# Order of 512- and 256-column products inside a weight unit of a feed-forward layer (two-layer streaming-encoder trunk, Trainium2)

## The chip, the cores and the metric

One core of one Trainium2 chip runs the whole program. The time is the device time of one execution in microseconds; smaller is better. It is the median of several executions. Engines are called as in the profile: PE (TensorE products), PEld (TensorE weight loads), DVE (VectorE), ACT (ScalarE), POOL (GpSimd), SP (the engine that issues most DMAs).

## The reference

A trunk of two layers over 256 positions of width 1024. Each layer has two feed-forward blocks, a token mixer between them and a gated embedding at the end; all matrices are float32.

```
def swiglu(x, w13, w2):
    gate, up = jnp.split(x @ w13, 2, axis=-1)
    return (jax.nn.silu(gate) * up) @ w2
...
    for i in range(DEPTH):
        h = h + 0.5 * rms_norm(swiglu(rms_norm(h, g[0]), ffn_w13[i, 0], ffn_w2[i, 0]), g[1])
        ...
        h = h + 0.5 * rms_norm(swiglu(rms_norm(h, g[4]), ffn_w13[i, 1], ffn_w2[i, 1]), g[5])
        ...
```

Between the two feed-forward blocks of a layer stands its token mixer, a gMLP in layer 0 and an RWKV-7 in layer 1. So there are four feed-forward blocks, each with a 1024 x 5632 matrix `w13` (gate and up halves) and a 2816 x 1024 matrix `w2`.

## The kernel before

**Precision by two parts.** A float32 operand is kept as a high part, rounded to the type fp32r, and a low part, the rest. A product of two such operands is made of three: high by high, low by high, high by low. Weights arrive from memory in units of 128 x 1024 (512 KB); ACT casts a unit to its high part (line 154), DVE subtracts that from the raw unit to get the low part (line 156). Both parts stand in one slot of 2048 columns: `need(i)` hands out `wh` and `wl`, `release(i)` gives the slot back. `pump` runs this splitting ahead of the products, up to 12 units.

**A feed-forward block** is the function `ffn`. The 2816 inner columns are cut into `FC` = 11 chunks `c` of 256. For the chunks 0 and 1 the products are made by `A` with the activations as stationary operand. For the chunks 2 to 10 the function `AT` makes them transposed, with the weights as stationary operand and the activations moving. `Dn(c, b)` then multiplies a chunk's result with `w2` for one half `b` of the positions: 12 products of 512 columns through `mm3` (lines 178, 179 and 180: high by high, low by high, high by low), three at a time into one of two PSUM banks called `acc`. The loop over `c` calls `AT(c)` and then, from the chunk two before, `Dn(c - 2, 0)` and `Dn(c - 2, 1)`.

**Inside `AT`** a chunk has two halves `j`, each with two PSUM banks `ps[0]` (gate) and `ps[1]` (up) and two weight units `u`. A unit holds four blocks `q` of 128 rows of the sum. The activations stand in `xs[u]` so that for each block the 256 columns of the high part (one for each position) are followed by the 256 of the low part. One product of the high weights with all 512 columns therefore gives high by high in `ps[i][:, :T]` and high by low in `ps[i][:, T:]`, and one of the low weights with the first 256 columns adds low by high to `ps[i][:, :T]` (`T` = 256). That is 16 products to a unit, eight of 512 columns (line 400) and eight of 256 (line 401), each with its own load of 128 stationary columns. After both units ACT copies the second halves of the banks out (line 408) and DVE adds the first halves (line 409); a scaling, the SiLU and the split of the result follow (lines 412 to 417).

The program has 4 blocks x 9 chunks = 36 calls of `AT`, 144 weight units in them, and 1152 pairs of a 512- and a 256-column product. The order of the products on PE is the order in which the code is written. Other places of the program show chains of products of one size: the gate product of the embedding and the `z` and `acc` products (512 columns), and the spatial product `s` of the gMLP (256 columns, 12 products in a row), all through `mm3`.

Of the kernel before, what the change touches and what calls it, by code (L numbers as in the profile page):

```python
# [16 lines left out]
T = 256  # L17
NB = 2
KT = 8
# [41 lines left out]
class Trunk:  # L61
# [264 lines left out]
    def ffn(self, l, j, at, filler=None):  # L326
        nc = self.nc
        at13, at2 = at
        gcol = l * 8 + 4 * j
        xs, xT, rstd = [], [], [None, None]  # L330
# [57 lines left out]
        def AT(c):  # L388


            for j in range(2):
                ps = [self.bank("mm") for _ in range(2)]
                for u in range(2):
                    wh, wl = self.need(at13[c] + 2 * j + u)
                    for q in range(4):
                        k = 4 * u + q
                        x = xs[u][:, q * 512:(q + 1) * 512]
                        for i in range(2):
                            sl = slice(q * 256 + i * 128, q * 256 + i * 128 + 128)
                            nc.tensor.matmul(ps[i], lhsT=wh[:, sl], rhs=x, start=k == 0, stop=False)  # L400
                            nc.tensor.matmul(ps[i][:, :T], lhsT=wl[:, sl], rhs=x[:, :T], start=False, stop=k == KT - 1)  # L401
                    self.release(at13[c] + 2 * j + u)
                self.pump(1, self.room)
                z = self.small(512, "pn", 3)
                sg = self.small(256, "k1", 6)
                for i in range(2):
                    zi = z[:, i * T:(i + 1) * T]
                    nc.scalar.copy(zi, ps[i][:, T:])  # L408
                    nc.vector.tensor_tensor(zi, ps[i][:, :T], zi, op=ALU.add)  # L409
                self.unbank(*ps)  # L410
                z2 = z.rearrange("p (i t) -> p i t", i=2)
                nc.vector.tensor_tensor(z2, z2, rbc.unsqueeze(1).to_broadcast([128, 2, T]), op=ALU.mult)  # L412
                nc.scalar.activation(sg, z[:, :T], AF.Silu)
                nc.vector.tensor_tensor(sg, sg, z[:, T:], op=ALU.mult)
                hi, lo = hv(c)[:, 0, j, :], hv(c)[:, 1, j, :]
                nc.scalar.copy(hi, sg)
                nc.vector.tensor_tensor(lo, sg, hi.bitcast(F32), op=ALU.subtract)
# [24 lines left out]
        for c in range(2, FC):  # L442
            AT(c); P(1)
            if c == 2:
                TR(1, 1)
            if c < FC - 1:
                Dn(c - 2, 0); P(2)
                if c < FC - 2:
                    Dn(c - 2, 1); P(1)
# [1151 lines left out]
```

## Time and profile before

| | us |
|---|---|
| runs | 1216.73, 1217.44, 1223.06 (median 1217.44) |
| the profiled execution, its own time | 1223.09 |
| its span, first to last instruction | 1221.2 |
| PE busy | 1188.6 (97% of the span) |
| DVE busy | 839.2 (69%) |
| ACT busy | 652.3 (53%) |
| mean granted TensorE clock | 0.981 of full speed |

The profiled execution has 1.9 us outside its span. A busy figure is the union of the records of an engine; since products are pipelined, their records overlap, and the time that one product adds to a chain is read from the start of one record to the start of the next, not from a record's length.

### The profile page before, as it was taken

What the parts mean: (1) busy time and instruction counts of PE and PEld (TensorE: products, weight loads), DVE (VectorE), ACT (ScalarE), POOL (GpSimd) and SP (SyncE); (2) the same over time, 40 slices, a digit from 0 to 9 for tenths busy, and PEclk for the clock granted to TensorE, in tenths of its full rate; (3) what the DMA queues carried; (4) which work ended last, traced back from release to release, by engine and by line L of the source; (5) the groups of instructions that cost most, each with busy time, mean ns of one, the idle gap of its engine ahead of it and who ended that gap; (6) DMA issues with size and microseconds to landing.
All of it is one profiled execution on the core that took longest, in us unless ns stands there. A gap on an engine that the chain in (4) does not pass through costs nothing. (4 is left out here: it accounts for less than half of the span.)

```text
span 1221.2 us, 18852 instructions
## 1 busy us (share of the span) xinstructions
PE 1188.6 (97%) x7374; PEld 966.8 (79%) x7374; DVE 839.2 (69%) x1273; ACT 652.3 (53%) x1122; POOL 97.7 (8%) x109
## 2 busy tenths in 40 slices
PE   8999999999999999999999999989899899999997
PEld 6888888888888888887888886576575778888886
DVE  5886666686787667668766744699253988666663
ACT  6665556454575555468655522472161377555553
POOL 0000001000010000012000001300025420000011
PEclk8999999999999999999999999999789899999999
DMA  7886655655767666555766672103020358656510
GB/s 245 293 282 190 191 171 163 234 173 189 220 209 231 191 186 187 188 171 167 242 183 196 189 281 98 50 4 138 3 93 19 121 194 273 198 183 192 171 58 35
DMA packets 58778, 207.73 MB, mean 170 GB/s; under 512 B 6720, under 2 KB 7232, under 8 KB 58432
## 3 DMA queue, kind: packets, MB, share of 16 engines
q1 hardware_dynamic: 58688, 206.51, 52.4%
q8 instruction: 58, 0.95, 0.3%
q14 instruction: 32, 0.26, 0.1%
HBM read 205.44 MB, written 1.05 MB: 169 GB/s over the span
## 5 line engine op out<-in xcount | busy, mean ns | idle before, releaser
L156 DVE TENSOR_TENSOR w<-raw,w 128x1024 fp32r<-128x1024 f32 x335 | 407.9, 1223 | 160.3 <-ACT w L154 154.8
L154 ACT CAST w<-raw 128x1024 fp32r<-128x1024 f32 x340 | 357.4, 1055 | 185.2 <-PE mm L401 76.2
L400 PE MATMUL mm<-xT,w 128*128 128x512 f32 x1152 | 408.5, 399 | 0.0
L401 PE MATMUL mm<-xT,w 128*128 128x256 f32 x1152 | 323.4, 281 | 0.0
L400 PEld LDWEIGHTS mm<-xT,w 128*128 128x128 f32 x1152 | 216.4, 188 | 53.4
L401 PEld LDWEIGHTS mm<-xT,w 128*128 128x128 f32 x1152 | 217.6, 189 | 1.3
L178 PE MATMUL acc<-w,hT 128*128 128x512 f32 x352 | 138.7, 394 | 0.0
L180 PE MATMUL acc<-w,hT 128*128 128x512 f32 x352 | 137.6, 391 | 0.0
L179 PE MATMUL acc<-w,hT 128*128 128x512 f32 x352 | 137.2, 390 | 0.0
L408 ACT COPY pn<-mm 128x256 f32<-128x256 f32 x144 | 48.6, 373 | 87.9 <-PE mm L401 87.9
L409 DVE TENSOR_TENSOR pn<-mm,pn 128x256 f32<-128x256 f32 x144 | 54.7, 420 | 36.1 <-ACT pn L408 36.1
L180 PEld LDWEIGHTS acc<-w,hT 128*128 128x128 f32 x352 | 66.1, 188 | 14.9
L178 PEld LDWEIGHTS acc<-w,hT 128*128 128x128 f32 x352 | 66.1, 188 | 13.9
L179 PEld LDWEIGHTS acc<-w,hT 128*128 128x128 f32 x352 | 66.2, 188 | 12.8
L232 POOL TENSOR_SCALAR rpost<-ss 128x1 f32<-128x1 f32 x15 | 7.4, 494 | 778.4 <-ACT junk L239 778.4
L178 PE MATMUL mm<-w,xT 128*128 128x512 f32 x128 | 51.6, 413 | 4.1 <-ACT w L154 3.7
L179 PE MATMUL mm<-w,xT 128*128 128x512 f32 x128 | 51.6, 406 | 0.7 <-DVE xT L289 0.5
L289 DVE SCALAR_TENSOR_TENSOR xT<-tr,gT,xT 128x128 fp32r<-128x128 f32 x112 | 35.7, 346 | 23.9 <-ACT xT L288 23.1
L180 PE MATMUL mm<-w,xT 128*128 128x512 f32 x128 | 51.1, 404 | 0.5 <-DVE w L156 0.5
L412 DVE TENSOR_TENSOR pn<-pn,yc 128x512 f32<-128x512 f32 x72 | 49.8, 691 | 2.1
L179 PE MATMUL z<-w,xT 128*128 128x512 f32 x128 | 49.9, 390 | 0.0
L180 PE MATMUL z<-w,xT 128*128 128x512 f32 x128 | 49.9, 390 | 0.0
(275 smaller groups left out, 1668.6 us busy)
## 6 DMA issues: line engine op xcount, KB each, us to landing
raw<-in_w SPq DMA_DIRECT2D x264, 512.0 KB, 4.3
raw<-in_win SPq DMA_DIRECT2D x32, 512.0 KB, 4.4
wf<-in_wrkv SPq DMA_DIRECT2D x12, 1024.0 KB, 6.0
raw<-in_wout SPq DMA_DIRECT2D x16, 512.0 KB, 4.6
raw<-in_wg SPq DMA_DIRECT2D x16, 512.0 KB, 3.8
gbc<-in_norm_g SPq DMA_DIRECT2D x9, 512.0 KB, 4.9
raw<-in_bwout SPq DMA_DIRECT2D x8, 512.0 KB, 3.5
bin<-in_bin SPq DMA_DIRECT2D x8, 256.0 KB, 5.3
```

The costliest lines, as they stand in the source:

```text
L154: self.high = self.nc.scalar.copy(hh, r[:p, :n])
L156: eng.tensor_tensor(ll, r[:p, :n], hh.bitcast(F32), op=ALU.subtract)
L178: mm(out, lhsT=lh, rhs=rh, start=start, stop=False)
L179: mm(out, lhsT=ll, rhs=rh, start=False, stop=False)
L180: mm(out, lhsT=lh, rhs=rl, start=False, stop=stop)
L232: nc.gpsimd.tensor_scalar(r, a, b, eps, op0=ALU.add, op1=ALU.add)
L289: nc.vector.scalar_tensor_tensor(lo, v, gc, hi.bitcast(F32), op0=ALU.mult, op1=ALU.subtract))
L400: nc.tensor.matmul(ps[i], lhsT=wh[:, sl], rhs=x, start=k == 0, stop=False)
L401: nc.tensor.matmul(ps[i][:, :T], lhsT=wl[:, sl], rhs=x[:, :T], start=False, stop=k == KT - 1)
L408: nc.scalar.copy(zi, ps[i][:, T:])
L409: nc.vector.tensor_tensor(zi, ps[i][:, :T], zi, op=ALU.add)
L412: nc.vector.tensor_tensor(z2, z2, rbc.unsqueeze(1).to_broadcast([128, 2, T]), op=ALU.mult)
```

## The change

Within a weight unit the loop over the two parts of the weights moves outward: first the high part with the four blocks and the two banks (eight products of 512 columns), then the low part with the same (eight of 256). No product, load, DMA or operation of another engine is added or taken away. The flags that begin and end a sum follow the first and last product of each bank.

```
-                    for q in range(4):
-                        k = 4 * u + q
-                        x = xs[u][:, q * 512:(q + 1) * 512]
-                        for i in range(2):
-                            sl = slice(q * 256 + i * 128, q * 256 + i * 128 + 128)
-                            nc.tensor.matmul(ps[i], lhsT=wh[:, sl], rhs=x, start=k == 0, stop=False)
-                            nc.tensor.matmul(ps[i][:, :T], lhsT=wl[:, sl], rhs=x[:, :T], start=False, stop=k == KT - 1)
+                    for s, w in enumerate((wh, wl)):
+                        for q in range(4):
+                            x = xs[u][:, q * 512:q * 512 + (T if s else 512)]
+                            for i in range(2):
+                                sl = slice(q * 256 + i * 128, q * 256 + i * 128 + 128)
+                                nc.tensor.matmul(ps[i][:, :T] if s else ps[i], lhsT=w[:, sl], rhs=x,
+                                                 start=u + q + s == 0, stop=s + u == 2 and q == 3)
```

On PE, the first weight unit of `AT` in the first block, before (`mm_392` and `mm_393` are the two banks, `w_275` the unit):

```order
L400 MATMUL mm_392<-xT_108,w_275 128x512
L401 MATMUL mm_392<-xT_108,w_275 128x256
L400 MATMUL mm_393<-xT_108,w_275 128x512
L401 MATMUL mm_393<-xT_108,w_275 128x256
L400 MATMUL mm_392<-xT_108,w_275 128x512
L401 MATMUL mm_392<-xT_108,w_275 128x256
```

Sizes alternate, and the bank is changed after every second product. The same unit, from its last two 512-column products into the next unit, with the change:

```order
L400 MATMUL mm_392<-xT_108,w_275 128x512
L400 MATMUL mm_393<-xT_108,w_275 128x512
L400 MATMUL mm_392<-xT_108,w_275 128x256
L400 MATMUL mm_393<-xT_108,w_275 128x256
L400 MATMUL mm_392<-xT_108,w_275 128x256
L400 MATMUL mm_393<-xT_108,w_275 128x256
L400 MATMUL mm_392<-xT_108,w_275 128x256
L400 MATMUL mm_393<-xT_108,w_275 128x256
L400 MATMUL mm_392<-xT_108,w_275 128x256
L400 MATMUL mm_393<-xT_108,w_275 128x256
L400 MATMUL mm_392<-xT_109,w_324 128x512
```

The size changes twice in a unit instead of sixteen times, and the bank changes after every product. On ACT only a few rows in the first `AT` of the program change places; there the cast of a later unit comes to stand ahead of the first copy out of the banks:

```order
 L154 CAST w_521<-raw 128x1024
+L154 CAST w_540<-raw 128x1024
 L408 COPY pn<-mm_392 128x256
-L154 CAST w_540<-raw 128x1024
 L408 COPY pn<-mm_393 128x256
```

The two copies now stand next to each other. DVE has the same few exchanges at the same place; SP and POOL have none.

## Rows read from the trace of the kernel before

**Rows 1.** The page: span, and busy time of each engine.
```profile
span 1221.2 us, 18852 instructions
...
PE 1188.6 (97%) x7374; PEld 966.8 (79%) x7374; DVE 839.2 (69%) x1273; ACT 652.3 (53%) x1122; POOL 97.7 (8%) x109
```

**Rows 2.** Stretches: length, busy time by engine (records), clock, DMA share, GB/s.
```profile
40.00:186.00 146.00, 146.00 (x773) 124.54 (x771) 108.94 (x153) 85.22 (x132) 1.05 (x1) 1.00 0.69 219
...
370.00:512.00 142.00, 142.00 (x753) 121.22 (x753) 98.28 (x139) 77.35 (x123) 0.00 (x0) 1.00 0.61 191
...
588.00:730.00 142.00, 142.00 (x753) 121.22 (x753) 91.82 (x133) 71.68 (x116) 0.00 (x0) 1.00 0.67 213
730.00:1022.00 292.00, 274.25 (x2743) 196.23 (x2741) 197.10 (x342) 125.12 (x243) 65.83 (x51) 0.94 0.27 92
1022.00:1165.00 143.00, 143.00 (x759) 122.12 (x758) 100.26 (x142) 79.59 (x126) 0.00 (x0) 1.00 0.62 197
```

**Rows 3.** The page's groups: the products of `AT`, and the loads (busy, mean ns | idle before).
```profile
L400 PE MATMUL mm<-xT,w 128*128 128x512 f32 x1152 | 408.5, 399 | 0.0
L401 PE MATMUL mm<-xT,w 128*128 128x256 f32 x1152 | 323.4, 281 | 0.0
...
L401 PEld LDWEIGHTS mm<-xT,w 128*128 128x128 f32 x1152 | 217.6, 189 | 1.3
```

**Rows 4.** PE in order of time, one whole `AT`: start us, length us, record.
```profile
56.64 0.39 PE L400 MATMUL mm<-xT,w 128*128 128x512 f32 x1
...
57.33 0.40 PE L400 MATMUL mm<-xT,w 128*128 128x512 f32 x1
57.57 0.28 PE L401 MATMUL mm<-xT,w 128*128 128x256 f32 x1
57.69 0.40 PE L400 MATMUL mm<-xT,w 128*128 128x512 f32 x1
...
61.57 0.40 PE L400 MATMUL mm<-xT,w 128*128 128x512 f32 x1
...
67.93 0.40 PE L178 MATMUL acc<-w,hT 128*128 128x512 f32 x1
```

**Rows 5.** PE in order of time, inside the gate product: 512 columns only.
```profile
538.57 0.39 PE L180 MATMUL gate<-w,xT 128*128 128x512 f32 x1
538.80 0.39 PE L178 MATMUL gate<-w,xT 128*128 128x512 f32 x1
...
541.29 0.39 PE L180 MATMUL gate<-w,xT 128*128 128x512 f32 x1
```

**Rows 6.** PE in order of time: 12 products of 256 columns between products of 512.
```profile
269.44 0.28 PE L178 MATMUL s<-vH,ws 128*128 128x256 f32 x1
269.56 0.28 PE L179 MATMUL s<-vH,ws 128*128 128x256 f32 x1
...
270.40 0.28 PE L180 MATMUL s<-vL,ws 128*128 128x256 f32 x1
...
270.88 0.40 PE L178 MATMUL z<-w,xT 128*128 128x512 f32 x1
271.11 0.40 PE L179 MATMUL z<-w,xT 128*128 128x512 f32 x1
...
272.94 0.39 PE L178 MATMUL z<-w,xT 128*128 128x512 f32 x1
```

**Rows 7.** PE in order of time: products of `Dn` behind that `AT`.
```profile
70.49 0.39 PE L180 MATMUL acc<-w,hT 128*128 128x512 f32 x1
70.71 0.39 PE L178 MATMUL acc<-w,hT 128*128 128x512 f32 x1
70.94 0.39 PE L179 MATMUL acc<-w,hT 128*128 128x512 f32 x1
...
71.39 0.39 PE L178 MATMUL acc<-w,hT 128*128 128x512 f32 x1
```

**Rows 8.** Waits of the whole run: who waited for whom, us in total, times, longest.
```profile
ACT pn L408 <- PE mm L401: 87.9, 66, 5.2
ACT w L154 <- PE mm L401: 76.2, 61, 2.1
...
PE mm L178 <- ACT w L154: 3.7, 1, 3.7
```

## The prediction

> **What bounds the kernel now.** I read the page's head first. PE is busy 1188.6 of 1221.2 us; DVE follows with 69% [rows 1]. That is an average, so I cut the span into stretches. Four of them hold nearly all the work that the change touches, the loops over the chunks 2 to 10 of the four feed-forward blocks. PE is busy there for 146.00 of 146.00, 142.00 of 142.00 (twice) and 143.00 of 143.00 us at a granted clock of 1.00, that is 2.4 GHz, while DVE has 92 to 109 us of work and the DMA engines are busy 61 to 69% [rows 2]. The groups say the same for the two lines that are reordered: not one of the 2304 products on the lines 400 and 401 had PE idle in front of it (0.0 in the last column) [rows 3]. Of PE's waits for a cast weight unit there is one, 3.7 us, at the activation-stationary products of `A` and not in `AT` [rows 8]. So inside `AT` the end of one product is what the next one waits for, and whatever the reordering does to the spacing of products goes straight into the time of that stretch.
>
> Now the spacing itself. A record's length (399 and 281 ns on average [rows 3]) is no price, since records overlap. I took start-to-start distances over many products, because rows are given to 0.01 us.
>
> - Alternating sizes, as in `AT` now: from 57.33 to 61.57 us twelve pairs start, 4.24 us, so 0.3533 us for a pair. Within a pair the 512-column product takes 0.24 us (57.33 to 57.57) and the 256-column one 0.12 (57.57 to 57.69) [rows 4].
> - Only 512 columns: from 538.57 to 541.29 us there are twelve steps, 2.72 us, so 0.2267 us each [rows 5].
> - Only 256 columns: from 269.56 to 270.88 us there are eleven steps, 1.32 us, so 0.1200 us each [rows 6].
>
> One product of each kind in a chain of its own kind is 0.2267 + 0.1200 = 0.3467 us. Mixed, the same two take 0.3533. The mixture costs 6.7 ns a pair, and it is the first of the two, the 512-column product, that is longer in it.
>
> **The change, part by part.** *What it does not touch.* The instructions are the same in number and kind: 1152 products of either size, as many loads, the same DMAs. A unit's slot is given back behind its last product as before, and casts that wait for a slot (76.2 us of ACT's waiting [rows 8]) stay where they are relative to the unit's end. The low part of a unit is now needed only after eight products (some 1.8 us later), which asks less of DVE; the whole high part is needed within those 1.8 us, but it is made by one cast, so its due time is the unit's first product as before. I put all this at zero; its cover is that PE has never waited for a unit in `AT`. The exchange of a few ACT and DVE rows in the first `AT` I cost at nothing for the same reason: what waits there are copies out of two banks that PE wants back only one half-chunk (two units, 5.6 us) later.
>
> *The spacing inside a unit.* Sixteen changes of size become two. Before, a unit is 8 x 0.3533 = 2.827 us. After, it is eight steps of 0.2267 and eight of 0.1200, 2.773 us, and the price of the two changes. Both changes stand in the trace, around the spatial product of the gMLP. Going from 512 to 256 columns, the first eight products of 256 take 269.44 to 270.40, 0.96 us, which is 8 x 0.1200: no price. Going back, the nine steps from 270.88 to 272.94 take 2.06 us, where nine in a long chain would take 2.04: a price of 0.02 us [rows 6]. So a unit becomes 2.793 us and saves 0.034. Times 144 units that is 4.8 us.
>
> *The products behind `AT`.* The first products of `Dn` are slower after the mixture too: fifteen steps from 67.93 to 71.39 take 3.46 us [rows 4, 7], where 15 x 0.2267 is 3.40. That tail of 0.06 us should become the 0.02 us that follows a chain of 256 columns. It saves 0.04 us in each of 36 calls, 1.4 us. (In four of the 36 transposes stand between; I count them all, the error is below 0.2 us.) The first unit of an `AT` comes from products of 512 columns and needs no way back, but the mixture also starts cheaply there: the whole `AT` takes 67.93 - 56.64 = 11.29 us where 32 x 0.3533 is 11.31 [rows 4]. These cancel, and I count neither.
>
> *Sum.* 4.8 + 1.4 = **6.2 us** less. Against the profiled execution, 1223.09 us, that gives 1216.9. That execution lies 5.65 us above the median of the runs shown, 1217.44; PE's half-clock time in the profile lies outside the four stretches (granted clock 0.94 from 730 to 1022 us [rows 2]) and may differ from run to run. Against the median the forecast is **1211.2 us**, 0.51% less.
>
> *Bounds.* If the change back to 512 columns costs nothing, a unit saves 0.053 us and the sum is 144 x 0.053 + 36 x 0.06 = 9.8 us. If it costs 0.04 us, as two readings of 0.01 us off would allow, a unit saves 0.013 and the sum is 144 x 0.013 + 36 x 0.02 = 2.6 us. I take 0.02, because it is the row's own value, and the row is the same two kinds of chain in the same order.
>
> **A rule against it.** By the rows a pair's price hangs on its neighbours: 0.3533 mixed, 0.3467 apart [rows 4 to 6]. The Trainium skill, TensorE: Matmul & The Clock Gate, section "Back-to-back issue gap", gives each product a gap by its own columns alone, 262 cycles for 256 and 518 for 512 at the full clock; by it a pair is an estimated 325 ns in any order and the sum is nothing. The trace does not agree with it on the size (353 ns) nor on the independence of the order, so I give it the chance of the first rival only.
>
> **Rivals.** *The order does not matter here.* The chains of one size in rows 5 and 6 have activations as the stationary operand or another matrix as the moving one, and three products in a row into one bank. In `AT` the stationary operand comes from a weight slot and all else differs too. If the 6.7 ns belong to those operands and not to the mixture, each pair keeps 0.3533 us and the time stays at 1217.4. For it: no chain of one size with `AT`'s own operands is in the trace. Against it: the slow tail in `Dn` after the mixture [rows 4, 7], which a property of `AT`'s operands would not leave behind. By what the rule above says the time would be this one as well.
>
> *Slower: the change of the bank costs.* Now the bank changes after every second product, afterwards after each one, 16 times in a unit instead of 8. If the 6.7 ns a pair are the price of its one change of bank, a unit becomes 2.773 + 16 x 0.0067 = 2.880 us, 0.053 more than now, and 144 units cost 7.7 us: 1225.1 us. It decides from about 4 ns for a change of bank, where eight more of them eat up the 0.034 us. Against it: in `Dn` the step from line 180 to line 178 enters the other bank and takes 0.22 us, the next one, in the same bank, 0.23 [rows 7].
>
> *The time comes back later.* The feed-forward blocks end 6 us sooner, and the stretch from 730 to 1022 us, where PE is busy 274 of 292 us [rows 2], might wait for something that does not come sooner. Three of the four blocks, 4.7 us of the 6.2, lie ahead of that stretch; losing their part leaves 1217.4 - 1.5 = 1215.9. Against it: its DMA share is 0.27, the lowest of all, and its waits are on chains that start from its own input.
>
> **How the numbers follow.** I give the forecast 0.72, the order that does not matter 0.12, the time given back later 0.08, the costly bank 0.08. About 0.5% (6.1 us) is what a measurement of this kernel can tell from no change, and the forecast's 6.2 us lies just on it. Of its 0.72 I put 0.44 on the far side of 6.1 us and 0.28 on the near side; with the two rivals of no or half an effect the near side has 0.48, and slower has 0.08. The likeliest case by its own bounds is 1207.6 to 1214.8. The range reaches from 1207.5 to 1218, where it takes in the case of no effect and leaves out the costly bank and odd runs.
>
> **What would show it.** In the profile after, PE's starts inside a unit should be 0.227 us apart for eight products and 0.12 us for eight, a unit some 2.79 us and an `AT` some 11.16 us from its first product to the first of `Dn`, with no idle time in front of line 400. The feed-forward stretches should be shorter by about 1.5 us each, the rest unchanged. I am wrong if a unit still takes 2.83 us (order neutral), if the steps of 512 columns are at or above 0.24 us throughout (bank), or if PE shows waits at line 400 for casts.

## The result, and the profile after

| | before | after |
|---|---|---|
| median us | 1218.34 (7 runs, 1216.73 to 1223.06) | 1211.93 (7 runs, 1210.16 to 1213.70) |
| profiled execution, own time | 1223.09 | 1211.93 |
| its span | 1221.2 | 1210.2 |

The changed kernel takes 0.994 of the time before, with a 95% interval of 0.9928 to 0.9952: 6.4 us less by the medians, where 6.2 were forecast. The predicted 1211.2 us stands 0.7 us from the measured median. (The forecast started from the median of the three runs known then, 1217.44; with seven it is 1218.34.)

The page of the changed kernel, span and busy times, and then the groups of the two kinds of product (both on line 400 now), with busy us, mean ns and idle time in front:

```profile
span 1210.2 us, 18850 instructions
...
PE 1178.6 (97%) x7374; PEld 966.2 (80%) x7374; DVE 838.5 (69%) x1273; ACT 648.8 (54%) x1122; POOL 97.2 (8%) x109
```

```profile
L400 PE MATMUL mm<-xT,w 128*128 128x512 f32 x1152 | 288.1, 392 | 0.0
L400 PE MATMUL mm<-xT,w 128*128 128x256 f32 x1152 | 160.6, 282 | 0.0
```

DVE and POOL have the work they had [rows 1]; ACT's busy time is 3.5 us lower with the same number of instructions. No product on line 400 finds PE idle before it, as before [rows 3]. The busy sums of the two groups fell from 408.5 and 323.4 to 288.1 and 160.6 us, and that is no saving: they are unions of overlapping records, and in the mixture the records of one kind alone, 399 ns long and one every 353 ns, already cover the whole time. PE's busy time on the page is 10.0 us lower; since PE is busy nearly throughout, that follows the span, with its scatter.

The stretches of the changed kernel (length, busy time by engine, clock, DMA share, GB/s), laid where the blocks' loops are now:

```profile
38.00:180.00 142.00, 142.00 (x762) 122.80 (x761) 105.84 (x150) 83.20 (x130) 0.89 (x1) 1.00 0.70 222
366.00:508.00 142.00, 142.00 (x762) 122.76 (x761) 99.59 (x140) 77.79 (x123) 0.00 (x0) 1.00 0.63 193
582.00:724.00 142.00, 142.00 (x762) 122.88 (x761) 93.11 (x134) 71.09 (x117) 0.00 (x0) 1.00 0.67 216
724.00:1005.00 281.00, 263.12 (x2702) 188.12 (x2701) 190.22 (x333) 120.19 (x237) 65.64 (x51) 0.95 0.26 88
1005.00:1154.00 149.00, 149.00 (x794) 128.49 (x794) 106.85 (x151) 83.52 (x131) 0.00 (x0) 1.00 0.64 202
```

The row from 724 us on is the stretch with the RWKV mixer, the other four hold the blocks. PE is still without a gap in the blocks, at the full clock, and DVE and DMA still have room [rows 2].

Where the time went, from PE's records in order of time. A block here reaches from its first product of `AT` to the first of `Dn` behind its last `AT`, block 4 from its third:

| | before | after |
|---|---|---|
| start to first block | 39.56 | 38.31 |
| block 1, 2, 3 (each) | 143.20 | 141.69 |
| block 4 | 142.84 | 141.25 |
| between 1 and 2 | 186.63 | 186.43 |
| between 2 and 3 | 74.56 | 73.98 |
| between 3 and 4 | 291.58 | 288.74 |
| behind 4 | 56.44 | 56.37 |

In block 4 the first two products of `AT` stand on PE some 7.5 us ahead of the third, among the products of `A` (1014.49 and 1021.94 us before, 1005.05 and 1012.54 after), so there the order on PE is not that of the code. Before they are a 512- and a 256-column product, 0.35 us, with the change two of 512, 0.45 us. With them block 4 takes 143.19 and 141.70 us, 1.49 less, and the four blocks are 3 x 1.51 + 1.49 = 6.0 us shorter.

The two spans differ by 11.0 us. Of the other 5 us, 4.2 lie in the start and in the stretch with the RWKV mixer. Both vary by themselves: over the ten traces of this study the start takes 36.1 to 39.6 us and the stretch between blocks 3 and 4 takes 287.8 to 291.8, with no order that follows the change (three traces whose blocks take the same 141.7 us have starts of 38.3, 38.0 and 36.8 us). In the start the length goes with TensorE's granted clock. Between 10 and 20 us, behind a first 10 us in which PE is busy for only 5.1 to 7.1, the clock is 0.66 to 0.74 in the six traces with a start of 37.46 us and more, and 0.83 in the four with a start of 36.83 us and less; such a mean is part of the time at 1.2 GHz and the rest at 2.4. The same window in the kernel before, then in the runs of two of the first experiment (length, busy time by engine, clock, DMA share, GB/s):

```profile
10.00:20.00 10.00, 9.11 (x28) 6.96 (x29) 6.46 (x11) 6.74 (x16) 0.87 (x2) 0.66 0.79 277
```

```profile
10.00:20.00 10.00, 9.73 (x39) 7.60 (x40) 7.51 (x15) 7.92 (x18) 0.87 (x2) 0.83 0.79 283
```

So the pair of profiles alone would have overstated the change by nearly a factor of two; the blocks state it: in the two orders that were profiled twice, the first three repeat to 0.01 us.

The spacing in an `AT` of the changed kernel, the one behind the chunk of rows 4 (start us, length us; a row `x2` stands for the first of two merged records):

```profile
71.90 0.39 PE L400 MATMUL mm<-xT,w 128*128 128x512 f32 x1
...
74.67 0.40 PE L400 MATMUL mm<-xT,w 128*128 128x512 f32 x1
74.90 0.40 PE L400 MATMUL mm<-xT,w 128*128 128x512 f32 x1
75.14 0.39 PE L400 MATMUL mm<-xT,w 128*128 128x512 f32 x1
...
76.51 0.40 PE L400 MATMUL mm<-xT,w 128*128 128x256 f32 x2
76.62 0.40 PE L400 MATMUL mm<-xT,w 128*128 128x256 f32 x2
...
77.46 0.40 PE L400 MATMUL mm<-xT,w 128*128 128x512 f32 x1
...
83.05 0.40 PE L178 MATMUL acc<-w,hT 128*128 128x512 f32 x1
83.28 0.40 PE L179 MATMUL acc<-w,hT 128*128 128x512 f32 x1
...
85.80 0.39 PE L178 MATMUL acc<-w,hT 128*128 128x512 f32 x1
```

The second unit runs from 74.67 to 77.46, 2.79 us: eight products of 512 columns in 1.84 and eight of 256 in 0.95. Eight of 512 in a long chain would take 1.81; the way back costs about 0.03, and the first products of 256 behind 512 give about 0.01 of it back. The `AT` takes 83.05 - 71.90 = 11.15 us, where it took 11.29 [rows 4], and the twelve steps of `Dn` behind it 2.75, where 12 x 0.2267 is 2.72.

### The profile page after: what moved, and what is told of

Its sections match the earlier page's. It is cut to its first block, busy times and chain, and to the rows that moved or that the text cites. A ratio compares the mean times of both kernels' runs of the same rounds, so it can differ in the third digit from the quotient of the medians.

```text
span 1210.2 us, 18850 instructions
## 1 busy us (share of the span) xinstructions
PE 1178.6 (97%) x7374; PEld 966.2 (80%) x7374; DVE 838.5 (69%) x1273; ACT 648.8 (54%) x1122; POOL 97.2 (8%) x109
## 5 line engine op out<-in xcount | busy, mean ns | idle before, releaser
L400 PE MATMUL mm<-xT,w 128*128 128x512 f32 (+1 forms) x2304 | 407.8, 337 | 0.0
L400 PEld LDWEIGHTS mm<-xT,w 128*128 128x128 f32 x2304 | 358.5, 189 | 50.1
L179 PE MATMUL z<-w,xT 128*128 128x512 f32 x128 | 50.0, 390 | 0.0
L180 PE MATMUL z<-w,xT 128*128 128x512 f32 x128 | 49.9, 390 | 0.0
L178 PE MATMUL z<-w,xT 128*128 128x512 f32 x128 | 49.6, 393 | 0.0
L288 ACT ACTIVATE xT<-tr,gT 128x128 fp32r<-128x128 f32 x112 | 37.8, 371 | 18.9 <-PE tr L275 14.5
```

Source lines behind the costliest of these rows:

```text
L178: mm(out, lhsT=lh, rhs=rh, start=start, stop=False)
L179: mm(out, lhsT=ll, rhs=rh, start=False, stop=False)
L180: mm(out, lhsT=lh, rhs=rl, start=False, stop=stop)
L288: done = (nc.scalar.activation(hi, v, AF.Copy, scale=gc), nc.vector.scalar_tensor_tensor(lo, v, gc, hi.bitcast(F32), op0=ALU.mult, op1=ALU ...
L400: nc.tensor.matmul(ps[i][:, :T] if s else ps[i], lhsT=w[:, sl], rhs=x, start=u + q + s == 0, stop=s + u == 2 and q == 3)
```

## The experiments

What is compared below is the time from the first product of an `AT` to the 13th product behind it (`AT` and its tail), since both ends lie in a settled chain of 512 columns. Without any price for mixing it would be 32 x 0.3467 + 12 x 0.2267 = 13.81 us; what lies above is the **excess**. Before it is 70.71 - 56.64 = 14.07 us, excess 0.26 [rows 4, 7]; after, 85.80 - 71.90 = 13.90 (13.893 as the mean of the 32 such places), excess 0.08. (36 calls less the first of each block, where transposes stand behind `AT`, leave 32.) The experiments reorder the 16 products of a unit, set the flags that begin and end a sum to match, and touch nothing else. Each code cut shows the line that sets the order.

### Runs of two

```
-                    for s, w in enumerate((wh, wl)):
-                        for q in range(4):
-                            ...
+                    order = [(s, q, i) for q in range(4) for s in range(2) for i in range(2)]
+                    for s, q, i in order:
...
```

> Runs of two: in a unit two products of 512 columns (one to each bank), then two of 256, four times over, so eight changes of size instead of two; the bank changes after every product, as in the changed kernel. Theory (price only at a change of size, built up over the products behind it): the first two 512-column products behind a run of 256 are 6 and 9 ns over 0.2267 us and the first 256 behind 512 is 7 ns under 0.12, so a unit is some 2.773 + 4 x 0.009 to 4 x 0.016 = 2.81 to 2.84 us, an AT 11.2 to 11.4 us, the time near that of the kernel before, 1216 to 1220. Rival (a fixed price of 0.021 us for every way back from 256 to 512): a unit is 2.856 us, an AT 11.4 us, 1222 us, slower than before. Rival (the bank order of the changed kernel is what helps, not the sizes): as the changed kernel, an AT of 11.15 us and 1212.

Measured: 1211.52 us median (4 runs), 0.9944 of before, 0.9923 to 0.9965. In order of time, runs of two:

```profile
86.22 0.39 PE L400 MATMUL mm<-xT,w 128*128 128x512 f32 x1
...
89.00 0.40 PE L400 MATMUL mm<-xT,w 128*128 128x512 f32 x1
89.47 0.40 PE L400 MATMUL mm<-xT,w 128*128 128x256 f32 x2
89.70 0.40 PE L400 MATMUL mm<-xT,w 128*128 128x512 f32 x1
90.17 0.39 PE L400 MATMUL mm<-xT,w 128*128 128x256 f32 x2
90.39 0.40 PE L400 MATMUL mm<-xT,w 128*128 128x512 f32 x1
...
91.79 0.40 PE L400 MATMUL mm<-xT,w 128*128 128x512 f32 x1
...
97.36 0.40 PE L178 MATMUL acc<-w,hT 128*128 128x512 f32 x1
...
100.09 0.39 PE L178 MATMUL acc<-w,hT 128*128 128x512 f32 x1
```

A unit takes 91.79 - 89.00 = 2.79 us with eight changes of size in it, no more than the changed kernel's with two. The `AT` takes 11.14 us, with its tail 13.87, excess 0.05. The theory as written failed: it took the first steps behind a long run of 256 (233 and 236 ns) as the price of any run, and these two steps are indeed there (89.00 to 89.47 is 0.47 us), but the pairs of 256 give most of the surplus back (89.47 to 89.70 is 0.23 and 90.17 to 90.39 is 0.22, where two steps of a long chain take 0.24). The rival of the fixed price failed by more. The figures of the rival of the bank order came out, so it took the next two runs to judge it.

### Runs of four

```
...
+                    order = [(s, 2 * p + q, i) for p in range(2) for s in range(2) for q in range(2) for i in range(2)]
...
```

> Runs of four: two blocks' products of 512 columns, then the same blocks' products of 256, twice in a unit, so four changes of size; the bank changes after every product. Theory: the first four 512-column products behind 256 cost 6 + 9 + 1 + 6 ns more and the first 256 some 7 less, so 0.016 us a change and back, a unit 2.773 + 2 x 0.016 = 2.805 us, an AT about 11.2 us, 1214 us, between the two kernels. Rival (fixed price of 0.021): a unit 2.815, 1215 us. Rival (bank order helps): as the changed kernel, 1212.

Measured: 1215.30 us median (10 runs), 0.9984 of before, 0.9969 to 0.9999. In order of time, runs of four:

```profile
87.84 0.39 PE L400 MATMUL mm<-xT,w 128*128 128x512 f32 x1
...
99.04 0.40 PE L178 MATMUL acc<-w,hT 128*128 128x512 f32 x1
...
101.80 0.39 PE L178 MATMUL acc<-w,hT 128*128 128x512 f32 x1
```

The `AT` takes 11.20 us and with its tail 13.97 (mean), excess 0.15: fewer changes of size than in runs of two, three times the excess. The theory's `AT`, about 11.2 us, came out; its 1214 us and the fixed price's 1215 the runs cannot tell apart, but a unit in the trace takes 2.807 us, where the theory had 2.805 and the fixed price 2.815. The bank changes after every product here too, as in the changed kernel, and the gain is not the changed kernel's, so the bank order is not what helps. The price does depend on the sequence of sizes, but not in proportion to the changes.

### The bank changed four times in a unit instead of sixteen

```
...
+                    order = [(s, q, i) for s in range(2) for i in range(2) for q in range(4)]
...
```

> The changed kernel with the loops over the bank and the blocks exchanged: four products of 512 columns into one bank, four into the other, then the same with 256 columns. The bank changes four times in a unit instead of sixteen, the size twice as in the changed kernel. Theory: the bank costs nothing, so a unit stays at 2.79 us, an AT at 11.15, the time at 1212 within 1 us. Rival (a change of bank has a price hidden under the gain, 1 to 4 ns each): a unit is 0.012 to 0.05 us shorter, 1205 to 1210 us.

Measured: 1212.51 us median (5 runs), 0.9953 of before, 0.9936 to 0.9969. In order of time, four products to a bank:

```profile
86.96 0.39 PE L400 MATMUL mm<-xT,w 128*128 128x512 f32 x1
...
98.10 0.40 PE L178 MATMUL acc<-w,hT 128*128 128x512 f32 x1
...
100.85 0.39 PE L178 MATMUL acc<-w,hT 128*128 128x512 f32 x1
```

The mean `AT` of the 32 is 11.146 us in both kernels, and with its tail 13.893 in both. A change of bank costs nothing that shows at this resolution. In this order no two neighbouring products share their moving operand, in the changed kernel the two products of each block `q` do; that makes no difference either.

### Alternating sizes, the neighbour in the other bank

```
...
+                    order = [(0, 0, 0)] + [p for n in range(7) for p in ((0, (n + 1) // 2, (n + 1) % 2), (1, n // 2, n % 2))] + [(1, 3, 1)]
...
```

> The kernel before with the 256-column products one place later: sizes still alternate nearly throughout a unit, but a 256-column product now goes to the other bank than the 512-column product ahead of it, and reads another stationary block. Theory (the alternation of sizes itself costs): the pairs keep 0.353 us, an AT stays at 11.25 to 11.3 us and the time at 1216 to 1219, as before. Rival (the price is that of two neighbouring products of unlike size into the same columns of one bank, the second adding to what the first still writes): pairs fall to 0.347 us, an AT to 11.1 us, 1211 us.

Measured: 1216.38 us median (10 runs), 0.9979 of before, 0.9968 to 0.9991. In order of time, the shifted alternation:

```profile
88.50 0.39 PE L400 MATMUL mm<-xT,w 128*128 128x512 f32 x1
...
99.77 0.40 PE L178 MATMUL acc<-w,hT 128*128 128x512 f32 x1
...
102.50 0.39 PE L178 MATMUL acc<-w,hT 128*128 128x512 f32 x1
```

The `AT` takes 11.27 us here (mean 11.264), with its tail 14.00, excess 0.19. Within a unit the pattern of the kernel before is back (start to start 232, 118, 241, 120, 236, 113 ns), although a 256-column product now follows one into the other bank. What it gains on the kernel before lies at the ends of the units, where two of a size meet (the excess is 0.19 in place of 0.26). So it isn't the bank and columns that a pair shares that cost.

### The second unit turned round

```
-                    for s, w in enumerate((wh, wl)):
+                    for s, w in ((0, wh), (1, wl))[::1 - 2 * u]:
...
-                                                 start=u + q + s == 0, stop=s + u == 2 and q == 3)
+                                                 start=u + q + s == 0, stop=s < u and q == 3)
```

> The changed kernel with the second unit of every half-chunk turned round: eight products of 512, eight of 256, then (next unit) eight of 256 and eight of 512. Sizes change half as often and an AT ends with 512 columns. Theory (a way back from a long run of 256 to a long run of 512 costs 0.02 us, nothing else does): an AT has two ways back in it instead of three, 11.147 - 0.021 = 11.126 us, and the products of Dn behind it lose their slow start of 0.027 us; together 36 x 0.048 = 1.7 us less than the changed kernel, 1210.2 us. Rival (the price hangs on the number of runs in a unit in some other way, as the cheap runs of two and the dear runs of four suggest): an AT within 0.02 us of 11.147 or longer, and no gain over the changed kernel.

Measured: 1211.52 us median (6 runs), 0.9939 of before, 0.9919 to 0.9958. In order of time, the turned-round unit:

```profile
89.27 0.39 PE L400 MATMUL mm<-xT,w 128*128 128x512 f32 x1
...
100.40 0.39 PE L178 MATMUL acc<-w,hT 128*128 128x512 f32 x1
...
103.12 0.39 PE L178 MATMUL acc<-w,hT 128*128 128x512 f32 x1
```

With its tail an `AT` takes 13.85 us, excess 0.04, half of the changed kernel's 0.08, and `Dn` starts at its settled pace at once (12 steps in 2.72). The forecast gain was 0.048 us an `AT`, 0.040 came. That is 1.4 us over 36, which the runs cannot tell from the changed kernel: measured beside it in the last experiment, the medians are 1211.52 and 1211.16.

### Runs of three

```
...
+                    order = [(s, n // 2, n % 2) for a, b in ((0, 3), (3, 6), (6, 8)) for s in range(2) for n in range(a, b)]
...
```

> Runs of three, three and two in a unit (six changes of size). Measured so far, the excess over 2.773 us for a unit: 0.053 in runs of one, 0.013 in runs of two, 0.034 in runs of four, 0.021 in runs of eight. Theory (the excess is a smooth function between neighbouring run lengths): 0.02 to 0.03 us, an AT of 11.16 to 11.2 us. Rival (it is a matter of where in a fixed pattern a run ends, even lengths up to two being cheap and odd ones dear): over 0.04 us, an AT of 11.22 us or more.

Measured: one run, 1215.24 us, too few for the time; the trace is read here. In order of time, runs of three:

```profile
87.08 0.39 PE L400 MATMUL mm<-xT,w 128*128 128x512 f32 x1
...
98.25 0.40 PE L178 MATMUL acc<-w,hT 128*128 128x512 f32 x1
...
100.98 0.39 PE L178 MATMUL acc<-w,hT 128*128 128x512 f32 x1
```

The `AT` takes 11.18 us, with its tail 13.91, excess 0.09, between runs of two and runs of four as the smooth guess had it. (The run is a mixture: each unit ends in a run of two.)

### Runs of two and the changed kernel again, beside the turned-round one

> The runs of two once more, on the same chip as the changed kernel and the turned-round one. By the traces (AT 11.138 against 11.147 us and no slow start of Dn behind it) it should be 36 x 0.03 = 1.1 us faster than the changed kernel, 1210.8; by the rival that such small differences are lost in other stages, equal to it.

> The changed kernel itself, as the yardstick for the two others of this set: 1211.9 us, ratio 0.994 to 0.995, AT 11.147 us by either theory.

Measured on one chip, six runs each: runs of two 1211.14 us, 0.9941 (0.9922 to 0.9961); the changed kernel 1211.16, 0.9939 (0.9922 to 0.9956). Together with the turned-round order three kernels lie within 0.4 us of each other by their medians. By the excess in their traces they should differ by 1.0 and 1.4 us over 36 calls; the 1.1 us forecast for the runs of two do not show. No order was found that beats the changed kernel by more than the runs can show.

| order in a unit | changes of size in it | `AT` with tail, us | excess | median us, ratio |
|---|---|---|---|---|
| alternating (before) | 16 | 14.07 | 0.26 | 1218.3, 1 |
| alternating, other bank | 14 | 14.00 | 0.19 | 1216.4, 0.9979 |
| runs of four | 4 | 13.97 | 0.15 | 1215.3, 0.9984 |
| runs of three | 6 | 13.91 | 0.09 | 1215.2 (one run) |
| runs of eight (after) | 2 | 13.89 | 0.08 | 1211.9, 0.9940 |
| runs of eight, fewer banks | 2 | 13.89 | 0.08 | 1212.5, 0.9953 |
| runs of two | 8 | 13.87 | 0.05 | 1211.5, 0.9944 |
| turned round | 1 on average | 13.85 | 0.04 | 1211.5, 0.9939 |

The times follow the excess: 36 times the difference of two rows is 6.5 us between the first and the changed kernel (6.4 measured), 3.8 us between before and runs of four (3.0 measured on their own chip), 2.6 and 1.9 for the shifted alternation. (It is a little too much, since the four calls with transposes behind them gain less: their `AT` fell by 0.12 us.) The single run of the runs of three stands apart: 6.0 us by the excess, 3.5 measured, in an execution whose stretch between blocks 3 and 4 is the longest of the ten, 291.8 us.

## Why the prediction was right

**PE sets the time of the blocks: shown.** Eight orders of the same instructions moved the blocks by their own spacing: in the order of the table a block takes 143.20, 142.58, 142.29, 141.83, 141.69, 141.69, 141.43 and 141.39 us. PE has no idle time in front of line 400 in the changed kernel, and of its waits for a cast unit there is one of 3.0 us, in `A`, in place of 3.7 [rows 8]. (A wait of 0.5 us for a low part, in `A` too, the prediction passed over; it is gone after.)

**The unit: 2.793 us forecast, 2.79 measured.** The way back from 256 to 512 columns was read from one place in the gMLP [rows 6], with other operands and another matrix. Taken to the nanosecond, the steps there behind the 256 are 233, 236, 228, 233, 231 and then 226 or 227 ns, and in the feed-forward blocks of the changed kernel they are the same within one. So the operands do not matter. The first rival falls, and with it the rule that the prediction set against itself, by which a pair takes the same time in any order: the same products in another order take 11.15 in place of 11.29 us.

**A piece of luck in it.** The prediction found no price from 512 to 256 columns and 0.02 us on the way back, both from rows of 0.01 us. To the nanosecond the same rows give 7 ns less than a long chain for the first eight products of 256 (the steps begin with 114 and 119 ns) and 27 ns more for the nine steps of 512. The two errors of reading cancel; the net 20 ns are right.

**The tail: 0.04 us a call forecast, 0.036 measured.** The twelve steps behind `AT` take 2.747 us now as the mean of the 32 places; before, they took 2.783 (70.71 - 67.93 = 2.78 [rows 4, 7]). What the prediction let cancel does: a whole `AT` is 0.02 us shorter than 32 mixed pairs before, and 0.03 shorter than four units of 2.793 us after.

**The sum: 6.2 us forecast, 6.0 in the blocks of the traces (without the tail behind each block's last `AT`, another 0.14), 6.4 by the medians.** The blocks were to be about 1.5 us shorter each, and they are. The whole gain arrived. The third rival, time given back later, falls: between the blocks nothing grew in the pair of traces, and the stretch with the RWKV mixer stays inside its own scatter.

**The costly bank falls** by two runs: sixteen changes of bank or four give the same `AT` to the nanosecond, and the alternation of sizes keeps its price when the neighbour goes to the other bank.

**The chances.** The forecast lay on the line of 0.5%, and 0.48 was put on its near side against 0.44 on the far one. The ratio of 0.994 lies on the far side, its interval (0.9928 to 0.9952) with nearly all its length. The mechanism and the size were forecast; the side of the line was not, and the chances leaned the wrong way. The scatter that made this a coin's toss is in the start and in the RWKV stretch.

**What the prediction did not know.** It treated the excess as a price for each way back. That is right for runs of eight and sixteen, and eight was the only case it needed. For shorter runs it fails: by 0.02 us for each way back a unit in runs of two would be 2.85 us, and it takes 2.79.

## What to carry to other kernels

Where PE never waits, read the start-to-start distance of its products over a dozen of them, in the mixture at hand and in places where one size stands alone; the difference is about what a reordering can give. Grouping equal column counts was worth 1.3% of an `AT` with its tail here, at no cost elsewhere that shows. Groups of eight and of two give it, groups of four only a part, so the order has to be measured; the number of changes does not tell it. Price such a change in the stretch it touches: the two single profiles differ elsewhere by 5 us, nearly as much as the whole gain.

## What was not expected of the hardware

The price of mixing sizes is not monotone in the length of the runs: excess 0.26 us in an `AT` with its tail for runs of one, 0.05 for two, 0.09 for three (with a run of two at the end of each unit), 0.15 for four, 0.08 for eight. The steps are a fixed pattern that repeats to a nanosecond from `AT` to `AT`; in these runs it depends on the sizes alone (not on the bank, not on whether neighbours share the moving operand). Each mean of `AT` with its tail, 14073.3, 14000.0, 13966.7, 13906.7, 13893.3, 13866.7 and 13853.3 ns, is a multiple of 6.67 ns to within the reading, and the settled steps of 226.7 and 120.0 ns differ by 106.7 ns, one column in each period of 2.4 GHz, and so both lie 13.3 ns above what 512 and 256 columns take at that rate. The sums hint at a common grid of 6.67 ns; the single steps in a mixture (113, 118, 232, 236, 241 ns) are no multiples of it, so products do not begin on such a grid. No run here shows where the pattern comes from; the mechanism stays open.
